# Feed-forward products of a two-block network as seven block products instead of eight, and SBUF tiles at multiples of 256 bytes

## The chip, the cores and the metric

The kernel runs on one core of a Trainium2 chip. The metric is the device time of one execution in microseconds (us), the median over the runs; lower is better.

## The reference, cut to what matters

The network is a block of state-space scan, attention and routed experts, followed by a second block of pooling, a second state-space mixer and a feed-forward part. All of it is float32 over 1024 tokens of 1024 channels. The change touches the very end:

```python
D_FF = 2816
def swiglu(h, w_gate, w_up, w_down):
    return (jax.nn.silu(h @ w_gate) * (h @ w_up)) @ w_down
...
h = h + jnp.concatenate([y_pool, y_ssm], axis=-1) @ w_out
h = h + swiglu(rmsnorm(h, norm_ffn), w_gate, w_up, w_down)
return rmsnorm(h, norm_final)
```

## The kernel before, in words

Float32 products are made on TensorE from operands in `float32r`. Each operand is split into a high part (a rounded copy, by ScalarE) and a low part (the operand minus its high part, by VectorE or GpSimd), and `mm3` (L194) issues three matmuls, high by high, high by low and low by high, into one PSUM bank. A product of a 128x128 block by 512 columns is so three matmuls of 128x512.

`out2` (L2341) is the last stage. Its first half, under `es2`, multiplies the mixer's output by `w_out` for two column halves `n`, adds the residual into `h` (eight row tiles of 128 tokens, in SBUF all the time), forms the mean square (`rms_part`, L1908), scales (`un`), and `split_T` (L1942) transposes each row tile into `hH` and `hL`: 8 blocks of 128 channels by 1024 tokens, high and low. These are the moving operand of what follows.

The second half is the feed-forward part. It takes the 22 column blocks in 11 pairs (`G = 2`). For each block `f`, `gate_up(f)` loads gate and up weights (two DMAs of 512 KB), splits them with the norm's gain folded in (ScalarE writes `gh`, VectorE `gl`), and 96 matmuls (2 token halves, gate and up, 8 channel blocks, 3 each) fill the banks `gu0` and `gu1`. ScalarE applies Silu, VectorE multiplies, ScalarE and GpSimd split the result into `xh` and `xl`. After a pair, 96 matmuls of the down product (8 row tiles, 2 column halves, 2 blocks, 3 each) go to `dn`, and VectorE adds each bank into `h` (L2438). In the last pair the final norm follows each row tile, and the rows leave by DMA.

So each token half sees the full product: gate and up take 22 x 96 = 2112 matmuls, down 11 x 96 = 1056.

The order of the work on each engine is fixed when the program is built: a list scheduler takes the instructions by the order of the source, and lets a later one go first where an earlier one waits for a buffer or an operand. A tile's buffers are a ring (`bufs`), and a new tile waits until the old one's readers are done. All loads of this stage are issued by SyncE's queue (SP), in order: a DMA that waits holds up those behind it.

`Lined` (L113) rounds the size of every SBUF tile up to a multiple of `LINE = 128` bytes, so that tiles start at multiples of 128 bytes. In the addresses that the program before was given, the tiles `h3H` and `h3L` start 128 bytes past a multiple of 256, while `gh`, `gl`, and the down product's `xh`, `xl`, `wh`, `wl` start at a multiple of 256. In the first half of `out2` `wh` and `wl` lie 128 past and `yh`, `yl` at a multiple; in the projection of the first block, `wh`, `wl`, `hH` and `hL` all lie 128 past.

Of the kernel before, what the change touches and what calls it, by code (L numbers as in the profile page):

```python
# [9 lines left out]
BF = mybir.dt.bfloat16  # L10
F = mybir.dt.float32
R = mybir.dt.float32r
# [9 lines left out]
D = 1024  # L22
# [13 lines left out]
def host_arrays(inp):  # L36
# [40 lines left out]
    col("norm_ffn", g["norm_ffn_2"][0].reshape(8, 128).T)  # L77
# [5 lines left out]
    put("ffn_gu", np.stack([g["w_gate_2"][0].reshape(8, 128, 22, 128), g["w_up_2"][0].reshape(8, 128, 22, 128)], 3).transpose(2, 1, 0, 3, 4))  # L83
# [29 lines left out]
class Lined:  # L113


    LINE = 128

    def __init__(self, pool):
        self.pool = pool

    def tile(self, shape, dtype, **kw):
        n, per = int(np.prod(shape[1:])), self.LINE // mybir.dt.size(dtype)
# [6 lines left out]
        return t.rearrange(f"p ({' '.join(names)}) -> p {' '.join(names)}", **dict(zip(names, shape[1:])))  # L129


class LinedContext:
# [8 lines left out]
    @contextmanager  # L141
    def tile_pool(self, **kw):
        with self.tc.tile_pool(**kw) as pool:
            yield pool if kw.get("space") in (PS, DR) else Lined(pool)


class Kernel:
# [60 lines left out]
    def run(self):  # L208
        nc, tc = self.nc, self.tc
        es = self.es  # L210
        with es:
            self.cst = es.enter_context(tc.tile_pool(name="cst", bufs=1))

            es.enter_context(tc.tc.tile_pool(name="edge", bufs=1, side="right")).tile([128, 8], F, name="edge")
# [2126 lines left out]
    def out2(self, y_es):  # L2341
        nc, tc, A = self.nc, self.tc, self.A
        V = nc.vector
        es = ExitStack()
        with es:
            pool = lambda name, bufs=1, **kw: es.enter_context(tc.tile_pool(name=name, bufs=bufs, **kw))
            hp = pool("h3", reuse_waits="tile")
            h = hp.tile([128, NB, D], F, name="h3")
            hH, hL = hp.tile([128, 8, L], R, name="h3H"), hp.tile([128, 8, L], R, name="h3L")
            ss = hp.tile([128, NB], F, name="ss")  # L2350
            gp = pool("ff_g", reuse_waits="tile")
            o_g = self.off["norm_ffn"][0]

            def gate_up(f, more=None):

                out = []
                for i in range(2):
                    st = gp.tile([128, 4, 256], F, name="gst", bufs=2)
                    nc.sync.dma_start(st, A["ffn_gu"][f].rearrange("p k g c -> p k (g c)")[:, 4 * i:4 * i + 4, :])
                    ring = (more, 1) if (2 * f + i) % 3 == 2 else (gp, 2)  # L2360
# [9 lines left out]
            with es2:  # L2370
# [3 lines left out]
                for n in range(2):  # L2374
                    s = slice(512 * n, 512 * n + 512)
                    wt = [self.wsplit(A["w_out_2"][k][:, s], whp, wlp, wsp, 512) for k in range(8)]
                    if n == 1:
                        g0 = gate_up(0)
# [105 lines left out]
```

## Time and profile before

| what | value |
|---|---|
| median of 3 runs | 2865.01 us (2856.89 to 2865.08) |
| the profiled execution's own time | 2855.95 us |
| its span | 2854.2 us |
| mean granted TensorE clock | 0.958 |
| busy in the span | PE 92%, PEld 72%, DVE 61%, ACT 44%, POOL 34% |
| DMA | 263.17 MB, mean 92 GB/s |

PE is TensorE's matmuls, PEld its weight loads, DVE VectorE, ACT ScalarE, POOL GpSimd. A matmul's busy time overlaps with the next one's, so the pace of the matmuls is read from the starts of successive ones, not from the time of one. The span runs from the first to the last instruction; the execution's own time is 1.75 us longer. "L196" is line 196 of the kernel; the three lines of `mm3` are L196, L197 and L198, and the names behind them tell the product apart.

### The profile page before, as it was taken

Reading aid. Unit: us, or ns where it says so; the run is one execution under the profiler, and the core shown is the slowest. Engines: PE = TensorE matmul, PEld = TensorE weight load, DVE = VectorE, ACT = ScalarE, POOL = GpSimd, SP = SyncE. Lnnn points to the kernel's source line nnn. Section 1 sums busy time; section 2 is a strip of 40 time slices with the busy share of each in tenths; the row PEclk is TensorE's granted clock in tenths of the full one; section 3 lists DMA queues with packets and bytes.
Section 4 is the critical chain, followed back from the end, with each engine's and each line's share of the span. In section 5 each row is a group of like instructions: output and inputs, shape, how many; then the busy total and the mean of one; then the engine's idle time right before and its main releaser. Section 6 shows DMA issues by size and latency. Waiting matters only on the chain.

```text
span 2854.2 us, 35834 instructions
## 1 busy us (share of the span) xinstructions
PE 2630.8 (92%) x12713; PEld 2067.2 (72%) x12713; DVE 1740.4 (61%) x3505; ACT 1260.7 (44%) x2748; POOL 968.3 (34%) x1059
## 2 busy tenths in 40 slices
PE   7799999988989999998979996869999999999998
PEld 4676788745777777777757775647878888888886
DVE  7655576797578898885566777596343333333334
ACT  3233444456369999983234553405341221111212
POOL 5522011273046666663344551044321111111111
PEclk9999999997999999999959998978999999999999
DMA  7555411001510000004167886311221111111111
GB/s 262 182 191 199 142 49 39 31 1 66 192 49 20 16 16 16 16 30 132 74 204 198 261 253 222 112 37 45 89 74 45 45 51 53 45 45 45 46 36 59
DMA packets 100388, 263.17 MB, mean 92 GB/s; under 512 B 16128, under 2 KB 36272, under 8 KB 91344
## 3 DMA queue, kind: packets, MB, share of 16 engines
q1 hardware_dynamic: 57792, 149.53, 15.2%
q0 software_dynamic: 14848, 70.67, 8.2%
q10 hardware_dynamic: 27568, 40.67, 4.2%
q8 instruction: 101, 1.65, 0.2%
q14 instruction: 79, 0.65, 0.1%
HBM read 212.55 MB, written 57.70 MB: 95 GB/s over the span
## 4 chain that ended last, share of the span: by engine, by line
PE 63%; DVE 16%; DMA 7%; ACT 6%; issue 5%; POOL 2%; SPq 0%; ACTq 0%; POOLq 0%; DVEq 0%
PE gu L196 6%; PE gu L198 6%; PE gu L197 6%; PE S L1116 4%; PE mm L196 4%; PE mm L197 4%; PE mm L198 4%; PE pt L1175 4%; PE dn L197 3%; PE dn L196 3%; PE dn L198 3%; ACT P L1151 2%; DMA u<-yo,tab 2%; PE pv L1196 2%; PE pv L1197 2%
## 5 line engine op out<-in xcount | busy, mean ns | idle before, releaser
L196 PE MATMUL gu<-h3H,gh 128*128 128x512 f32 x704 | 279.0, 396 | 0.0
L198 PE MATMUL gu<-h3H,gl 128*128 128x512 f32 x704 | 278.7, 396 | 0.0
L197 PE MATMUL gu<-h3L,gh 128*128 128x512 f32 x704 | 278.7, 396 | 0.0
L1184 DVE TENSOR_TENSOR pl<-pt,ph 128x512 fp32r<-128x512 f32 x320 | 219.2, 686 | 51.5 <-ACT ph L1180 46.2
L1151 ACT ACTIVATE P<-S,hd 128x512 f32<-128x512 f32 (+1 forms) x384 | 237.6, 622 | 1.8 <-DVE hd L1136 1.8
L1166 POOL TENSOR_SCALAR P<-P,hd 128x512 f32<-128x512 f32 (+1 forms) x256 | 201.8, 801 | 91.0 <-DVE hd L1164 86.4
L1116 PE MATMUL S<-kS,qS 128*128 128x512 f32 (+1 forms) x768 | 211.5, 372 | 19.0 <-ACT P L1151 19.0
L1180 ACT CAST ph<-pt 128x512 fp32r<-128x512 f32 x320 | 187.4, 586 | 28.2 <-PE pt L1175 15.2
L1175 PE MATMUL pt<-consts,P 128*128 128x128 f32 x1280 | 192.9, 273 | 6.5 <-DVE pl L1184 5.4
L2365 DVE SCALAR_TENSOR_TENSOR gl<-gst,vcol,gh 128x256 fp32r<-128x256 f32 x176 | 93.2, 580 | 169.3 <-ACT gh L2364 168.5
L202 POOL TENSOR_TENSOR xl<-sa,xh 128x512 fp32r<-128x512 f32 x44 | 58.0, 1319 | 406.2 <-ACT xh L2427 406.2
L1175 PEld LDWEIGHTS pt<-consts,P 128*128 128x128 f32 x1280 | 156.5, 140 | 45.1 <-DVE pl L1184 9.2
L1129 DVE TENSOR_REDUCE mx<-S 128x1 f32<-128x512 f32 x256 | 173.9, 680 | 2.9 <-PE S L1116 2.2
L2438 DVE TENSOR_TENSOR h<-h,dn 128x512 f32<-128x512 f32 x176 | 119.6, 684 | 89.7 <-PE dn L198 89.7
L964 POOL TENSOR_TENSOR wl<-wst,wh 128x1024 fp32r<-128x1024 f32 (+1 forms) x42 | 84.6, 2024 | 264.3 <-ACT wh L963 263.8
L1116 PEld LDWEIGHTS S<-kS,qS 128*128 128x128 f32 x768 | 128.5, 190 | 63.0 <-ACT P L1151 42.8
L2426 DVE TENSOR_TENSOR sa<-sa,gu 128x512 f32<-128x512 f32 x44 | 30.2, 686 | 234.0 <-PE gu L198 234.0
L197 PEld LDWEIGHTS gu<-h3L,gh 128*128 128x128 f32 x704 | 132.7, 189 | 32.1
L196 PEld LDWEIGHTS gu<-h3H,gh 128*128 128x128 f32 x704 | 132.8, 189 | 32.0
L198 PEld LDWEIGHTS gu<-h3H,gl 128*128 128x128 f32 x704 | 132.6, 188 | 32.1
L1196 PE MATMUL pv<-ph,vS 128*128 128x512 f32 x320 | 150.5, 470 | 1.7 <-ACT ph L1180 1.1
L581 DVE SCALAR_TENSOR_TENSOR acc<-cv,vcol,acc 128x254 f32<-128x254 f32 (+5 forms) x288 | 110.2, 433 | 53.0 <-ACT acc L583 50.5
(690 smaller groups left out, 6941.8 us busy)
## 6 DMA issues: line engine op xcount, KB each, us to landing
gst<-in_ffn_gu_dram SPq DMA_DIRECT2D x44, 512.0 KB, 3.5
wmod<-in_w_mod_dram ACTq DMA_DIRECT2D x64, 256.0 KB, 3.8
wst<-in_ffn_down_dram SPq DMA_DIRECT2D x22, 512.0 KB, 3.9
wst<-in_w_in_dram SPq DMA_DIRECT2D x40, 256.0 KB, 4.0
wmod<-in_w_mod_a_dram SPq DMA_DIRECT2D x8, 1024.0 KB, 5.2
qT<-qt ACTq DMA_DIRECT2D x16, 512.0 KB, 4.3
wst<-in_w_out_dram SPq DMA_DIRECT2D x16, 512.0 KB, 5.4
qS<-qT SPq DMA_DIRECT2D x8, 1024.0 KB, 4.9
```

The source lines that it names most:

```text
L196: nc.tensor.matmul(out, lh, rh, start=first, stop=False)
L197: nc.tensor.matmul(out, lh, rl, start=False, stop=False)
L198: nc.tensor.matmul(out, ll, rh, start=False, stop=last)
L1116: nc.tensor.matmul(S[:, o:o + z - a], qS[b][:, 4 * j + 2 * p + e, :], kS[4 * m + j][:, a:z], start=m == 0, stop=m == 1)
L1129: V.tensor_reduce(m[:, k // 3, k % 3:k % 3 + 1], bank[n], axis=AX.X, op=OP.max)
L1151: nc.scalar.activation(x, bank[n][:, o:o + z - a], AF.Exp, bias=neg[h], accum_out=tot[h][:, i:i + 1])
L1166: nc.gpsimd.tensor_scalar(P[h, half], P[h, half], r[:, 0:1], 1.0, op0=OP.mult, op1=OP.mult)
L1175: nc.tensor.transpose(pt[:, i, :], P[4 * g + i, int(c > 3)][:, o:o + 128], self.ident)
L1180: nc.scalar.copy(split[n][1], split[n][0])
L1184: V.tensor_sub(split[n][2], split[n][0], split[n][1])
L1196: nc.tensor.matmul(pv, v, ph, start=c == 0, stop=False)
L2438: V.tensor_add(x[:, s], x[:, s], ps)
```

## The change

Gate, up and down are each cut into 2 x 2 blocks and computed by seven block products in Winograd's form of Strassen's scheme. For gate and up, the left matrix has the rows (gate, up) of one column block and the columns (channels 0 to 511, 512 to 1023); the right one is the normed input with the channels and the token halves. For down, the left matrix is the hidden layer cut by token half and by column block of a pair, and the right one `w_down` cut by block of a pair and by output half.

- `out2` keeps only its first half. The gain of the norm moves from the weights into `un` (one scalar_tensor_tensor of 128x1024 instead of a tensor_scalar). The transposed input goes into four pairs of tiles `B[i, n]`. `h` is stored to DRAM (`h3`), one DMA of 512 KB per row tile.
- `ffn_hidden` runs blocks 0 and 1 with the eight products (`plain`), and during these forms the sums of input blocks (`sums`, `third`: 48 VectorE operations of 128x512). Blocks 2 to 21 run `operands` and `seven`. Every second block, `pair` forms the left sums for down on GpSimd and stores seven operands (256 KB each), and `weights` loads two rows of `w_down` blocks, forms the right sums on GpSimd and stores them.
- `ffn_out` loads for each of the seven products and each of the 11 pairs two operands of 256 KB, splits them, and accumulates over the 11 pairs in four banks; the banks are then added into the row tiles `y`, which start as `h3`.
- The layout of `ffn_gu` in DRAM changes so that each of the four blocks of a column block is one DMA of 256 KB.
- `Lined.LINE` becomes 256 for every SBUF tile of the kernel; tiles of up to 2048 bytes that are no multiple of it go to a pool of their own, which is filled up to a multiple.

```diff
 class Lined:
-    LINE = 128
+    LINE = 256
+    SMALL = 2048
...
+        if n % per and n * size <= self.SMALL:
+            self.taken[kw["name"]] = kw.get("bufs", self.bufs) * -(-n * size // 32) * 32
+            return self.small.tile(shape, dtype, **kw)
...
 def out2(self, y_es):
-                                V.tensor_scalar(un, x, r, None, op0=OP.mult)
-                                self.split_T(pp, un, hH, hL, t, 2)
+                                nc.sync.dma_start(self.h3[t], x)
+                                V.scalar_tensor_tensor(un, x, r, gain, op0=OP.mult, op1=OP.mult)
+                                turned(un, t)
...
+    def ffn_split(self, x, pool):
+        hi, lo = (pool.tile([128, 4, 128], R, name=n) for n in ("gh", "gl"))
+        flat = lambda t: t.rearrange("p a b -> p (a b)")
+        self.nc.scalar.copy(flat(hi), x)
+        self.nc.vector.tensor_sub(flat(lo), x, flat(hi))
+        return hi, lo
...
+            bp, yp, gy, pp = pool("ff_b"), pool("ff_y"), pool("ff_h", 4), pool("ff_ps", 8, space=PS)
+            T = {t: [bp.tile([128, 4, 512], R, name=f"t{t}{x}") for x in "hl"] for t in (1, 2, 4)}
+            T[3] = B[0, 1]
+            def product(ps, op, b, first, last):
+                for k in range(4):
+                    self.mm3(ps, op[0][:, k, :], op[1][:, k, :], b[0][:, k, :], b[1][:, k, :], first and k == 0, last and k == 3)
...
+            def operands(f):
+                a11, a21, a12 = (self.ffn_raw(f, gp, *gi) for gi in ((0, 0), (1, 0), (0, 1)))
+                a22 = self.ffn_raw(f, gy, 1, 1, bufs=1)
+                s2, s3 = buf("s2"), buf("s3")
+                ops = {}
+                ops[1] = self.ffn_split(a11, gy)
+                V.tensor_sub(s3, a11, a21)
+                V.tensor_sub(s2, a22, s3)
+                ops[6] = self.ffn_split(s2, gp)
+                ops[7] = self.ffn_split(s3, gy)
+                V.tensor_add(a21, a21, a22)
+                ops[5] = self.ffn_split(a21, gp)
+                ops[2] = self.ffn_split(a12, gy)
+                ops[4] = self.ffn_split(a22, gp)
+                V.tensor_sub(s2, a12, s2)
+                ops[3] = self.ffn_split(s2, gy)
+                return ops
+            def seven(f, ops):
+                y = [buf(f"h{f % 2}{n}") for n in range(2)]
+                p1, u2, u3, x = (buf("u", 8) for _ in range(4))
...
+                nc.scalar.copy(p1, prod(1, B[0, 0]))
+                V.tensor_add(u2, p1, prod(6, T[2]))
+                V.tensor_add(u3, u2, prod(7, T[3]))
+                m5 = prod(5, T[1])
+                V.tensor_add(u2, u2, m5)
+                V.tensor_add(x, u3, m5)
+                V.tensor_add(p1, p1, prod(2, B[1, 0]))
+                nc.scalar.activation(p1, p1, AF.Silu)
+                V.tensor_add(u3, u3, prod(4, T[4]))
+                V.tensor_mul(y[0], p1, u3)
+                V.tensor_add(u2, u2, prod(3, B[1, 1]))
+                nc.scalar.activation(u2, u2, AF.Silu)
+                V.tensor_mul(y[1], u2, x)
+                return y
+            def pair(i, h0, h1):
+                (a11, a21), (a12, a22) = h0, h1
+                nc.gpsimd.tensor_sub(s3, a11, a21)
+                nc.gpsimd.tensor_add(a21, a21, a22)
+                nc.gpsimd.tensor_sub(s2, a22, s3)
+                nc.gpsimd.tensor_sub(s4, a12, s2)
+                for p, x in enumerate((a11, a12, s4, a22, a21, s2, s3)):
+                    nc.sync.dma_start(self.hop[11 * p + i][:], x)
+            def weights(i):
...
+            for f in range(2, 22):
+                ops = operands(f)
+                if f % 2 == 0:
+                    i = f // 2 - 1
+                    pair(i, hid.pop(f - 2), hid.pop(f - 1))
+                    weights(i)
+                hid[f] = seven(f, ops)
...
+    def ffn_out(self):
+            sp, op = pool("fd_s", 6), pool("fd_o", 11)
...
+            def operands(p, i):
...
+                nc.scalar.copy(hi, st)
+                V.tensor_sub(lo, st, hi)
...
+            for t in range(NB):
+                nc.sync.dma_start(y[t], self.h3[t])
+            product(1, (0, 1), (1, 0), (1, 1), (0, 0))
+            product(6, (0, 1), (1, 0), (1, 1))
+            product(5, (0, 1), (1, 1))
+            product(3, (0, 1))
+            product(2, (0, 0))
+            for t in range(4):
+                final(t)
+            product(7, (1, 0), (1, 1))
...
```

Product 4 comes last; it runs row tile by row tile, each followed by the final norm of that tile.

## Rows read from the trace of the kernel before

**Rows 1.** The page: busy tenths of TensorE in 40 slices of the span.

```profile
PE   7799999988989999998979996869999999999998
```

**Rows 2.** Stretches: busy us (instructions) of PE, PEld, DVE, ACT, POOL; clock, DMA share, GB/s.

```profile
2200.00:2300.00 100.00, 100.00 (x434) 81.27 (x433) 33.72 (x57) 19.28 (x38) 12.68 (x9) 1.00 0.15 48
...
2000.00:2010.00 10.00, 10.00 (x44) 8.10 (x43) 4.31 (x7) 2.55 (x4) 0.14 (x1) 1.00 0.87 318
2100.00:2110.00 10.00, 5.91 (x20) 4.78 (x19) 5.97 (x16) 4.63 (x10) 0.44 (x1) 0.67 0.71 227
```

**Rows 3.** Timeline of PE: start, duration (us), operands; one pair of the feed-forward part.

```profile
2307.49 0.40 PE L196 MATMUL gu<-h3H,gh 128*128 128x512 f32 x1
...
2352.29 0.39 PE L196 MATMUL dn<-wh,xh 128*128 128x512 f32 x1
...
2374.06 0.40 PE L196 MATMUL gu<-h3H,gh 128*128 128x512 f32 x1
```

**Rows 4.** The same of unbroken runs: 102 matmuls of a projection, 93 of out2.

```profile
136.29 0.40 PE L196 MATMUL mm<-wh,hH 128*128 128x512 f32 x1
...
159.23 0.39 PE L198 MATMUL mm<-wh,hL 128*128 128x512 f32 x1
...
2048.74 0.39 PE L196 MATMUL mm<-wh,yh 128*128 128x512 f32 x1
...
2070.11 0.40 PE L198 MATMUL mm<-wh,yl 128*128 128x512 f32 x1
```

**Rows 5.** Groups, 2200 to 2790 us: busy us, mean ns; idle before, releaser.

```profile
L2438 DVE TENSOR_TENSOR h<-h,dn 128x512 f32<-128x512 f32 x144 | 98.0, 685 | 78.2 <-PE dn L198 78.2
L202 POOL TENSOR_TENSOR xl<-sa,xh 128x512 fp32r<-128x512 f32 x36 | 47.7, 1324 | 334.7 <-ACT xh L2427 334.7
L2425 ACT ACTIVATE sa<-gu 128x512 f32<-128x512 f32 x35 | 20.9, 597 | 144.2 <-PE gu L198 144.2
L963 ACT CAST wh<-wst 128x1024 fp32r<-128x1024 f32 x18 | 18.0, 1050 | 171.8 <-PE dn L198 171.8
```

**Rows 6.** Groups of DVE over the whole span: two inputs in SBUF, 512 and 1024 columns.

```profile
L1611 DVE TENSOR_TENSOR gul<-wst,guh 128x1024 fp32r<-128x1024 f32 x64 | 75.7, 1222 | 40.7 <-ACT guh L1610 39.3 <-DMA s_k<-oT 1.2
...
L2390 DVE TENSOR_TENSOR yl<-yc,yh 128x512 fp32r<-128x512 f32 x16 | 11.0, 692 | 27.2 <-ACT yh L2389 27.1
```

**Rows 7.** Timeline of DVE and of POOL around 1993 us.

```profile
1993.65 1.75 DVE L2336 TENSOR_TENSOR yc<-yc,th 128x512 f32<-128x512 f32 x1
...
1993.56 1.29 POOL L964 TENSOR_TENSOR wl<-wst,wh 128x512 fp32r<-128x512 f32 x1 [0.23 <-ACT wh L963]
```

**Rows 8.** Timeline of DVE: the next block's weights and the product of the current block.

```profile
2327.60 1.69 DVE L2365 SCALAR_TENSOR_TENSOR gl<-gst,vcol,gh 128x256 fp32r<-128x256 f32 x4 [7.96 <-ACT gh L2364]
2330.16 0.69 DVE L2426 TENSOR_TENSOR sa<-sa,gu 128x512 f32<-128x512 f32 x1 [0.87 <-PE gu L198]
```

**Rows 9.** One DMA issue of SP (start, us), and issues: count, size, us to landing.

```profile
2106.35 0.33 SPq L2359 DMA_DIRECT2D gst<-in_ffn_gu_dram  x1
...
wst<-in_w_in_dram SPq DMA_DIRECT2D x40, 256.0 KB, 4.0
```

**Rows 10.** Timeline at the start of the feed-forward part.

```profile
2103.48 0.75 DVE L2401 TENSOR_SCALAR gst<-h,rr 128x1024 f32<-128x1024 f32 x1
...
2105.97 0.78 PE L196 MATMUL gu<-h3H,gh 128*128 128x512 f32 x1
...
2108.68 0.63 PE L196 MATMUL gu<-h3H,gh 128*128 128x512 f32 x1
```

**Rows 11.** The end: timeline, and the group of the final norm's squares.

```profile
2840.55 0.40 PE L198 MATMUL dn<-wh,xl 128*128 128x512 f32 x1
...
2848.32 0.20 ACT L187 ACTIVATE qs<-rv 128x1 f32<-128x1 f32 x1 [3.82 <-DVE rv L2446]
...
2849.50 1.42 DVE L2458 SCALAR_TENSOR_TENSOR wst<-h,qo,gfin 128x512 f32<-128x512 f32 x2
...
L2444 ACT ACTIVATE junk<-h 128x1024 bf16<-128x1024 f32 x4 | 4.2, 1053 | 3.9 <-DVE h L2438 3.2 <-DVE qr L188 0.7
```

More of the change, by code (lines that the diff above doesn't have):

```diff
@@ L129, in tile, with fill @@
         return t.rearrange(f"p ({' '.join(names)}) -> p {' '.join(names)}", **dict(zip(names, shape[1:])))
+    def fill(self):
+        rest = -sum(self.taken.values()) % self.LINE
+        if rest:
+            self.small.tile([128, rest // 4], F, name="fill", bufs=1)
 class LinedContext:
@@ L2343, in out2 @@
         V = nc.vector
+        self.h3 = self.dram.tile([NB, 128, D], F, name="h3d")
         es = ExitStack()
         with es:
[L2346 to L2360, printed above, removed]
-                    gh, gl = (ring[0].tile([128, 4, 256], R, name=x, bufs=ring[1]) for x in ("gh", "gl"))
-                    for k in range(4):
-                        gm = self.vcol[:, o_g + 4 * i + k:o_g + 4 * i + k + 1]
-                        nc.scalar.activation(gh[:, k, :], st[:, k, :], AF.Copy, scale=gm)
-                        V.scalar_tensor_tensor(gl[:, k, :], st[:, k, :], gm, gh[:, k, :], op0=OP.mult, op1=OP.subtract)
-                    out.append((gh, gl))
-                return out
+            hp = es.enter_context(tc.tile_pool(name="h3", bufs=1, reuse_waits="tile"))
+            B = {(i, n): [hp.tile([128, 4, 512], R, name=f"b{i}{n}{x}") for x in "hl"] for i, n in ((0, 0), (1, 0), (1, 1), (0, 1))}
+            gp = es.enter_context(tc.tile_pool(name="ff_g", bufs=3, reuse_waits="tile"))
             es2 = ExitStack()
@@ L2373, in out2, with turned @@
                 wsp, whp, wlp = pool2("o2_s", 2, reuse_waits="tile"), pool2("o2_h", 8, reuse_waits="tile"), pool2("o2_l", 8, reuse_waits="tile")
+                h = wp.tile([128, NB, D], F, name="h3")
+                ss = wp.tile([128, NB], F, name="ss")
+                gain = self.row(wp, "gain", A["norm_ffn"])
+                def turned(x, t):
+                    for i in range(2):
+                        pt = pp.tile([128, 4, 128], F, name="tp", bufs=2)
+                        for j in range(4):
+                            k = 4 * i + j
+                            nc.tensor.transpose(pt[:, j, :], x[:, 128 * k:128 * k + 128], self.ident)
+                        hi, lo = (b[:, :, 128 * (t % 4):128 * (t % 4) + 128] for b in B[i, t // 4])
+                        nc.scalar.copy(hi, pt)
+                        V.tensor_sub(lo, pt, hi)
                 for n in range(2):
```

210 lines of the change are left out of this document (146 added, 64 removed).

## The prediction, made blind

> **What bounds the kernel now.** I read the busy slices of the page first: from the slice at about 1930 us TensorE stands at nine tenths up to the last slice [rows 1]. The stretches in numbers come next: in 100 us of the feed-forward part PE is busy for all of it at the full clock (1.00, the 2.4 GHz level), while VectorE has 34 us, ScalarE 19, GpSimd 13, and DMA a share of 0.15 [rows 2]. No other engine sets the pace there, so a matmul taken out gives back its own spacing. That spacing is read from the starts of matmuls [rows 3]: 192 gate and up matmuls take 2352.29 - 2307.49 = 44.80 us, 0.2333 each, and the 96 of down 2374.06 - 2352.29 = 21.77 us, 0.2268 each. Both are 128x512 in the same type and at the same clock. In sum, 2112 x 0.2333 + 1056 x 0.2268 = 732.2 us; from the first of these matmuls at 2105.97 [rows 10] to the start of the last at 2840.55 [rows 11] there are 734.6. The missing 2.4 us lie at the start: six intervals from 2105.97 to 2108.68 take 2.71 us instead of 1.40 [rows 10], at the lower clock after PE stood idle for some 4 us (granted 0.67 over that stretch, [rows 2]). After the last matmul's start 13.65 us remain to the end of the span.
>
> **Why two spacings.** By the addresses of the program before, gate and up stream `h3H` and `h3L` (128 bytes past a multiple of 256) against weights at a multiple; down has both at a multiple. Two other runs separate the address from the product [rows 4]: with both operands 128 past, 101 intervals take 22.94 us, 0.2271 each; with the moving one 128 past and the other at a multiple, 92 intervals take 21.37 us, 0.2323 each. Equal residues run at 0.227, unequal ones at 0.232 to 0.233. With `LINE = 256` all large tiles have residue 0, so I take 0.2268 for every matmul of the new stage; the other end is 0.2333.
>
> The Trainium skill, "SBUF — State Buffer", section "Who interferes with whom", speaks against this: PE never waits on anyone there, and it has independent read ports for the two operands. By that rule an address could not matter, and gate and up would keep 0.2333. The rows of this trace side with the address, but by two pairs only; that is a rival below.
>
> **The change, part by part.**
>
> *Matmuls.* Gate and up: 2 blocks x 96 + 20 x 7 products x 12 = 192 + 1680 = 1872. Down: 7 products x 11 pairs x 4 tiles x 3 = 924. In all 2796 for 3168. At 0.2268: 634.1 us for 732.2, so -98.1 (fewer matmuls give -84 to -87 of it, the spacing the rest).
>
> *Supply of a block of gate and up.* Its 84 matmuls take 19.05 us. VectorE has 4 sums, 7 low parts and 9 steps from the banks: 20 x 0.69 [rows 5, 6] = 13.8 us. ScalarE has 7 copies, one evacuation and 2 Silu: 10 x 0.60 [rows 5] = 6.0. Both lie under the 19.05, provided that the operands of a block are made while the one before it multiplies. The rings allow that: seven split operands stand in rings of four and three, in the order of the products, so the first of the next block can be split when product 1 of this one is done. That the scheduler uses such room is seen in [rows 8]: `gl` of the next block runs 2.6 us before the last multiplication of the current one, although it stands later in the source. So cost 0; with the cover gone it is the slower rival below.
>
> *GpSimd.* Per pair of blocks 8 sums of 128x512 at 1.32 [rows 5] = 10.6 us of 38.1. Two results meet a deadline: the store of `a21` must have landed before `y[1]` of the next block overwrites it, 19 us after the last product of the pair; three sums (4 us), the issue and the landing (4.0, [rows 9]) leave over 10 us. Cost 0, bounds 0 and the rival on the port.
>
> *SP's queue.* Per pair of blocks 8 loads, 7 stores and 4 larger transfers, 19 issues of 0.33 us [rows 9] in 38 us, 6.0 MB, 158 GB/s. In the down part two loads of 256 KB per four tiles' 12 matmuls (2.72 us): 193 GB/s. The trace has moved 318 GB/s in a stretch [rows 2]. A store that waits for GpSimd holds up the loads behind it, at most for the 10.6 us of the sums; the raw weights are a block ahead of their use, so nothing of it reaches PE.
>
> *Start.* `un` as a two-input operation takes 1.22 [rows 6] for 0.75 [rows 10] on the last tile's chain: +0.5. During blocks 0 and 1 (43.5 us of PE) VectorE has 48 operations of sums, 4 multiplications, 5 low parts and 11 operations of block 2: 68 x 0.69 = 46.9 us, 0.61 to 0.65 each where they run back to back. Bounds 0 and 8 us of stall at block 2; I take 2, near the difference.
>
> *Into down.* The first six operand buffers lie where `B[0,0]` and `B[1,0]` lay, free after products 1 and 2 of the last block, so the first pairs are loaded before its end. The row tiles (8 x 512 KB = 4.2 MB, 13 us at 318 GB/s) stand ahead of the later operands in SP's queue. With six pairs (16 us of PE) loaded, bounds are 0 and 9 us (a load of 4.0, copy 1.05 and low part 1.22 [rows 5, 6], and some 2 us at the low clock); I take 4. Within down VectorE has per product 11 low parts x 1.22 + 8 additions x 0.69 = 18.9 of 29.9 us: cost 0.
>
> *End.* Before, the last pair ends on four row tiles whose norms queue on VectorE. Now each of the last four tiles has 33 matmuls, 7.5 us, so only the last tile's chain stands behind PE: addition 0.69, square 1.05 [rows 11], 1.4 for the mean square and the root (1.2 of it from 2848.32 to 2849.50), two products with the gain 1.42, 3.3 from their end to the end of the span [rows 11], 0.39 of the last matmul and 0.7 of hand-overs: 9.0 for 13.65, so -4.7.
>
> *The stages ahead.* The 384 matmuls of `out2`'s first half go from 0.2323 to 0.2268: -2.1. For other stages the new addresses and the new order of buffers may do either; I take 0, bounds -10 and +8.
>
> Sum: 2105.97 - 2.1 + 0.5 + 634.1 + 2.4 + 2 + 4 + 9.0 = 2755.9 us of span, and 1.75 around it: 2757.6, 98 us under the profiled execution's 2855.95. That execution lies 9.1 us under the median (two of three runs are at 2865, one at 2857), so I add a little: 2760.
>
> **The rivals.**
>
> *The port of GpSimd and VectorE binds.* In [rows 7] an operation of VectorE with two SBUF inputs takes 1.75 us instead of 0.69, begun 0.09 us after one of GpSimd that takes 1.29. Eleven of a block's 20 VectorE operations have two SBUF inputs. If each of the 8 GpSimd sums held VectorE throughout, a pair of blocks would need 27.6 + 10.6 = 38.2 us of VectorE against 38.1 of PE: no slack left. Then half a hold (0.65) reaches PE per sum: 8 x 0.65 x 10 pairs = 52 us as a ceiling, 26 as a middle: 2786, up to 2812. For it: the collision is in the trace. Against: nine operations read PSUM, and the operands stand a block ahead. The Trainium skill has the rule, same page and section: the two-input operation and the GpSimd one exclude each other for the whole instruction. The trace agrees with it (1.75 for 0.69).
>
> *The address does nothing.* Then gate and up cost 1872 x 0.0065 = 12 us more and `out2` keeps its 2: 2774.
>
> *The operands are not made ahead: slower.* If VectorE takes a block's sums and splits only behind the last evacuation of the block before, PE waits at each of 20 blocks for addition 0.69, Silu 0.60, multiplication 0.69, copy 0.60 and low part 0.69 = 3.3 us, some 1.5 more at products 6 and 5, and pays the low clock afterwards, 2.0 [rows 10]: 6.8 x 20 = 136 us: 2896. The gain is 98 us, 4.9 per block, and above that the change loses. For it: the rings are just seven deep, and `s2` has a single buffer for two of the operands. Against: [rows 8].
>
> **How the numbers follow.** Forecast 2760: 0.63, its own range 2740 to 2780. Port: 0.15. Address: 0.12. Operands late: 0.10, nearly all of it slower. The range 2738 to 2815 holds the first three and leaves out the last. One measurement tells no change from 0.3% (8.6 us) or more; so faster 0.90, same 0.02, slower 0.08.
>
> **What would show it.** Matmuls of gate, up and down all 0.227 apart; about 425 us from the first matmul of block 0 to the last of block 21, and 210 for down; PE at 1.00 in both but for gaps of some us at block 2 and at the first of down; VectorE at about 0.7 of the hidden part; 9 us behind the last matmul. Gaps at each block would be the late operands, gaps beside GpSimd's sums the port, a spacing of 0.233 the address.

## The result and the profile after

The changed kernel takes 2810.36 us (median of 4 runs, 2808.94 to 2832.09), the kernel before 2861.34 beside it (4 runs, 2856.89 to 2865.08). The ratio is 0.9843, 95% interval 0.9808 to 0.9878. It is 51 us or 1.6% faster where the prediction had 100 us, though 2810 lies inside the range given. The profiled run takes 2809.2 us with a span of 2807.3, of which 51.4 are more than the 2755.9 of the prediction's sum.

Execution times of one kernel spread here by up to 33 us. In the profiles of after and its variants the feed-forward part begins anywhere from 2101.6 to 2132.1 us, so much of the spread arises ahead of it (last section). So the parts are compared by their own length, from the start of the first feed-forward matmul to the end of the span: 748.2 us before (2105.97 to 2854.2), 701.9 after (2105.47 to 2807.3), 651.5 in the forecast.

TensorE's busy tenths on the page, in answer to [rows 1]:

```profile
PE   7899999998999999998978996887987999997998
```

Slices 31 (from 2105 us) and 37 (from 2527 us) stand at seven tenths, where before has nine. The stretches, with the columns of [rows 2]:

```profile
2100.00:2150.00 50.00, 46.12 (x196) 38.33 (x197) 28.52 (x37) 10.43 (x19) 24.76 (x17) 0.91 0.60 215
2150.00:2200.00 50.00, 29.75 (x101) 21.60 (x99) 34.25 (x50) 12.74 (x23) 34.54 (x15) 0.78 0.50 173
...
2300.00:2400.00 100.00, 100.00 (x443) 82.82 (x442) 80.21 (x112) 33.58 (x57) 19.84 (x12) 1.00 0.36 116
...
2565.00:2620.00 55.00, 38.64 (x136) 29.48 (x135) 24.36 (x23) 22.82 (x23) 4.69 (x3) 0.81 0.91 330
2650.00:2750.00 100.00, 100.00 (x442) 82.80 (x442) 63.52 (x87) 44.56 (x50) 0.00 (x0) 1.00 0.60 199
```

Where PE is busy for all of the stretch, 443 matmuls go into 100 us for 434 before [rows 2]. VectorE takes 80 us of 100 there for 34. Two stretches are far from full: 2150 to 2200, where GpSimd is busy for 34.5 of 50 us, and 2565 to 2620, where the DMA engines have a share of 0.91 and move 330 GB/s.

The 2796 matmuls of the part are 0.2267 us apart wherever they follow each other closely (2704 intervals of 0.2267 on average). What an interval takes beyond that is called lost here: a wait, or a matmul at a lower clock behind one (the two stretches above have a granted clock of 0.78 and 0.81; behind the waits matmuls are 0.43 apart). In after 59.9 us are lost, for 8.4 in the forecast (2.4 + 2 + 4): 1.9 in block 0, 0.0 in block 1, 21.2 in block 2, 8.8 in block 3, 3.3 in blocks 4 to 21, 4.9 in the step into down, 19.8 in down's first product, and nothing in the six products behind it.

**Blocks 2 and 3.** What PE waited for from 2150 to 2260 (us in total, times, longest), the last row from 2564 to 2620:

```profile
PE m L217 <- DVE gl L2434: 8.0, 3, 5.4
PE m L215 <- ACT gh L2433: 7.0, 2, 6.1
PE m L215 <- ACT t2h L2481: 5.6, 1, 5.6
...
PE a L215 <- ACT oh L2609: 16.1, 3, 8.2
```

The late operands are split parts (`gh`, `gl`) and the sum of right operands `t2`. VectorE makes `gl` and the sums that ScalarE then rounds to `gh` and `t2h`, and GpSimd's timeline shows what stands beside it:

```profile
2137.50 1.29 POOL L2562 TENSOR_TENSOR d<-d 128x512 f32<-128x512 f32 x1 [5.36 <-DMA d<-in_ffn_down_dram]
...
2163.16 9.55 POOL L2562 TENSOR_TENSOR d<-d 128x512 f32<-128x512 f32 x1 [4.80 <-DMA d<-in_ffn_down_dram]
2172.78 7.13 POOL L2563 TENSOR_TENSOR d<-d,d 128x512 f32<-128x512 f32 x1
...
2182.93 1.29 POOL L2550 TENSOR_TENSOR h<-h,h 128x512 f32<-128x512 f32 x1
```

`d` are the down weights of `weights(i)`. Nothing in them depends on the hidden layer, so they did not stay where the loop has them: all eleven sets run from 2100 to 2257 us, by the end of block 5 (one of the expectations below says nine of eleven; it is all). VectorE's timeline:

```profile
2106.83 0.68 DVE L2388 TENSOR_TENSOR b11l<-tp,b11h 128x512 fp32r<-128x512 f32 x1
2118.54 0.69 DVE L2498 TENSOR_TENSOR h<-u,m 128x512 f32<-128x512 f32 x1 [11.03 <-PE m L217]
...
2122.23 0.69 DVE L2472 TENSOR_TENSOR u<-b01h,b01l 128x512 f32<-128x512 f32 x1
...
2136.96 0.68 DVE L2482 TENSOR_TENSOR t2l<-u,t2h 128x512 fp32r<-128x512 f32 x1
2137.56 1.78 DVE L2479 TENSOR_TENSOR u<-u,b10l 128x512 f32<-128x512 f32 x1
2139.27 1.78 DVE L2472 TENSOR_TENSOR u<-b01h,b01l 128x512 f32<-128x512 f32 x1
...
2183.84 0.68 DVE L2535 TENSOR_TENSOR u<-u,m 128x512 f32<-128x512 f32 x1
2197.42 0.69 DVE L2509 TENSOR_TENSOR s<-gst 128x512 f32<-128x512 f32 x1 [12.89 <-DMA gst<-in_ffn_gu_dram]
```

Three things are to be seen. The right operand is complete at 2107.5, but the first sum of it (L2472) runs at 2122.2: it stands in VectorE's fixed order behind block 0's product `h` (L2498), which waits 11 us for PE. From 2137.5, beside GpSimd, an operation takes 1.78 us for 0.68, as in [rows 7]. And the wait works in the other direction too: at 2163 to 2180, where VectorE has operation behind operation, GpSimd's two take 9.55 and 7.13 for 1.29. SP's queue shows what follows:

```profile
2158.81 2.78 SPq L2560 DMA_DIRECT2D d<-in_ffn_down_dram  x2
2179.93 3.38 SPq L2567 DMA_DIRECT2D wop<-d  x2
...
2192.18 1.88 SPq L2427 DMA_DIRECT2D gst<-in_ffn_gu_dram  x3
```

The store of `d` (`wop`) waits for GpSimd until 2179.9, and the loads of block 3's weights (`gst`) stand behind it until 2192.2. VectorE waits 12.89 us for them, and PE 6.5 at 2193.7.

**Into down.** SP's queue, then ScalarE's copies of the operands:

```profile
2564.18 0.32 SPq L2554 DMA_DIRECT2D hop<-h  x1
2564.60 0.38 SPq L2606 DMA_DIRECT2D st<-hop  x1
...
2567.40 1.71 SPq L2554 DMA_DIRECT2D hop<-h  x2
2572.30 0.80 SPq L2554 DMA_DIRECT2D hop<-hs  x2
2573.14 0.45 SPq L2607 DMA_DIRECT2D st<-in_ffn_down_dram  x1
...
2575.34 6.87 SPq L2648 DMA_DIRECT2D y<-h3d  x8
2583.19 0.32 SPq L2606 DMA_DIRECT2D st<-hop  x1
```

```profile
2568.85 1.04 ACT L2609 CAST oh<-st 128x1024 fp32r<-128x1024 f32 x1 [2.20 <-DMA st<-in_ffn_down_dram]
2577.02 1.04 ACT L2609 CAST oh<-st 128x1024 fp32r<-128x1024 f32 x1 [7.13 <-DMA st<-in_ffn_down_dram]
2580.09 1.05 ACT L2609 CAST oh<-st 128x1024 fp32r<-128x1024 f32 x1 [2.02 <-DMA st<-in_ffn_down_dram]
2593.56 1.04 ACT L2609 CAST oh<-st 128x1024 fp32r<-128x1024 f32 x1 [12.43 <-DMA st<-in_ffn_down_dram]
```

The first load of an operand (`st`) is issued at 2564.6, when block 21 issues its last matmuls: SP stood at a store of that block's `y[0]` (`hop<-h`). The two loads of the second pair are parted by four more stores of the last pair. After the third pair come the eight row tiles, and the fourth pair's operand is copied at 2593.56, 12.4 us after ScalarE was free for it.

**The end.** In answer to [rows 11], the last matmul and the last tile's products with the gain:

```profile
2798.98 0.39 PE L217 MATMUL a<-oh,ol 128*128 128x512 f32 x1
...
2802.74 1.41 DVE L2632 SCALAR_TENSOR_TENSOR un<-y,qo,gfin 128x512 f32<-128x512 f32 x2
```

From the last matmul's start to the end of the span it is 8.35 us for 13.65.

### The profile page after: what moved, and what is told of

Read it like the earlier page. It is cut to its first block, busy times and chain, and to the rows that moved or that the text cites. A ratio compares the mean times of both kernels' runs of the same rounds, so it can differ in the third digit from the quotient of the medians.

```text
span 2807.3 us, 36195 instructions
## 1 busy us (share of the span) xinstructions
PE 2550.4 (91%) x12341; PEld 2007.4 (72%) x12341; DVE 1976.1 (70%) x3707; ACT 1324.0 (47%) x2762; POOL 1002.0 (36%) x1078
## 5 line engine op out<-in xcount | busy, mean ns | idle before, releaser
L1135 PE MATMUL S<-kS,qS 128*128 128x512 f32 (+1 forms) x768 | 211.7, 373 | 18.2 <-ACT P L1170 18.2
L2610 DVE TENSOR_TENSOR ol<-st,oh 128x1024 fp32r<-128x1024 f32 x77 | 92.8, 1221 | 65.9 <-ACT oh L2609 62.0
L215 PE MATMUL a<-oh 128*128 128x512 f32 x308 | 122.3, 400 | 16.1 <-ACT oh L2609 16.1
L1216 PE MATMUL pv<-pl,vS 128*128 128x512 f32 x320 | 126.8, 396 | 0.2 <-DVE pl L1203 0.2
L216 PE MATMUL a<-ol,oh 128*128 128x512 f32 x308 | 122.7, 398 | 0.2 <-DVE ol L2610 0.2
L217 PE MATMUL a<-oh,ol 128*128 128x512 f32 x308 | 122.2, 397 | 0.0
L216 PE MATMUL mm<-wl,hH 128*128 128x512 f32 x288 | 114.6, 398 | 1.4 <-DVE wl L255 1.1
L215 PE MATMUL mm<-wh,hH 128*128 128x512 f32 x288 | 115.5, 401 | 0.0
L217 PE MATMUL mm<-wh,hL 128*128 128x512 f32 x288 | 113.5, 394 | 0.0
L217 PE MATMUL cv<-hH,wl 128*128 128x512 f32 (+1 forms) x288 | 104.2, 362 | 1.0 <-POOL wl L584 1.0
L215 PE MATMUL cv<-hH,wh 128*128 128x512 f32 (+1 forms) x288 | 105.0, 364 | 0.0
```

The costliest lines, as they stand in the source:

```text
L215: nc.tensor.matmul(out, lh, rh, start=first, stop=False)
L216: nc.tensor.matmul(out, lh, rl, start=False, stop=False)
L217: nc.tensor.matmul(out, ll, rh, start=False, stop=last)
L1135: nc.tensor.matmul(S[:, o:o + z - a], qS[b][:, 4 * j + 2 * p + e, :], kS[4 * m + j][:, a:z], start=m == 0, stop=m == 1)
L1216: nc.tensor.matmul(pv, v, pl, start=False, stop=c == NBT - 1)
```

## The experiments

The table gathers what the profiles show: the length from the first feed-forward matmul to the end, and the us lost by stretch (as above, beyond 0.2267 us between the starts of matmuls; in shifted the 6.1 of blocks 4 to 21 are the wider spacing and no waits).

| kernel | length | blocks 0, 1 | 2 | 3 | 4 to 21 | step | 1st product | behind PE |
|---|---|---|---|---|---|---|---|---|
| forecast | 651.5 | 2.4 | 2 | 0 | 0 | 4 (both) | | 9.0 |
| after | 701.9 | 1.9 | 21.2 | 8.8 | 3.3 | 4.9 | 19.8 | 8.3 |
| sums_early | 692.5 | 9.0 | 9.1 | 0 | 9.8 | 4.3 | 17.9 | 8.8 |
| weights_held | 686.9 | 0.7 | 10.2 | 0 | 9.8 | 10.9 | 13.6 | 8.3 |
| weights_queue | 708.8 | 2.0 | 14.8 | 21.4 | 5.5 | 4.7 | 18.2 | 8.5 |
| no_weights | 671.9 | 2.1 | 5.2 | 0 | 0 | 4.5 | 18.1 | 8.5 |
| vector_sums | 666.0 | 0.7 | 4.0 | 0 | 0 | 4.5 | 14.9 | 8.3 |
| rows_late | 693.7 | 2.0 | 18.4 | 8.1 | 1.2 | 4.4 | 7.6 (+10.2 in the 2nd) | 8.3 |
| quarters | 693.7 | 1.8 | 14.8 | 21.1 | 1.5 | 4.5 | 7.6 | 8.9 |
| pool_stores | 682.8 | 1.5 | 20.8 | 8.7 | 1.7 | 2.5 | 5.8 | 8.2 |
| all_three | 655.7 | 1.9 | 4.1 | 0 | 0 | 2.5 | 5.0 | 8.7 |
| shifted | 660.9 | 2.5 | 2.0 | 0.3 | 6.1 | 2.6 | 5.2 | 8.7 |
| last_steps | 648.6 | 1.8 | 0 | 0 | 0 | 2.5 | 2.5 | 8.2 |

**The addresses alone (line_only).** The kernel before with the changed allocator:

```diff
-    LINE = 128
+    LINE = 256
...
+        if n % per and n * size <= self.SMALL:
...
+            return self.small.tile(shape, dtype, **kw)
```

> The kernel before, with tiles at multiples of 256 bytes and nothing else of the change (same products, same order). The address theory: the 2112 gate and up matmuls go from 0.2333 to 0.2268 us apart and the 384 of the first half of the output product before them from 0.2323 to 0.2268, 13.7 + 2.1 = 16 us in all, so some 2845 for 2861 (ratio 0.9945), with spacings of 0.227 everywhere. The rival, that the spacing belongs to the product and not to the addresses: 0.2333 stays, ratio 1.000.

Measured: 2833.13 us (2832.17 to 2835.74), ratio 0.9916 (0.9883 to 0.9949). The part takes 733.5 us for 748.2: 14.7 less, and the gate and up matmuls are 0.2273 apart on average. From the first matmul of out2 to the feed-forward part 127.3 us pass for 129.4, the 2.1 expected. Of the rest of the 25 us, 7 lie ahead of out2 in the profiled runs, before 1830 us; whether the addresses or the spread between executions gave them is open. The address theory holds: with the products of before, the allocator alone gives 14.7 us in the part, for the 46.3 of all of after.

**The sums of the right operands first (sums_early).**

```diff
-            hid[0] = plain(0, four(0, g0))
-            g1 = four(1, self.ffn_three(1, gp))
+            f0 = four(0, g0)
             sums(t3)
+            hid[0] = plain(0, f0)
+            g1 = four(1, self.ffn_three(1, gp))
```

> The kernel after, with the sums of the right operands ordered ahead of block 0's products (and of block 1's splits), so that VectorE begins them when the last transposed tile is complete, at about 2108 and not at 2122. If VectorE's order is the cause, most of block 2's 21 us goes: 14 to 21 us gained, 2790 to 2796, and block 3 keeps its gap. If GpSimd's early sums on the port are the cause, the sums start earlier but run at 1.75 us beside GpSimd, and the gain is 0 to 7 us.

Measured: 2811.83 us (2795.15 to 2817.02), ratio 0.9819 (0.9774 to 0.9864): no gain that can be told from after. Block 2 loses 12 us less, but 7 appear in blocks 0 and 1 and 7 in blocks 4 to 21. In the part's length 9.4 us are gained, and block 3's gap, expected to stay, is gone. With GpSimd at work the order moves the loss rather than taking it away.

**The weights held back (weights_held).** Each `weights(i)` is ordered behind the stores of its pair:

```diff
-                    pair(i, hid.pop(f - 2), hid.pop(f - 1))
-                    weights(i)
+                    last = pair(i, hid.pop(f - 2), hid.pop(f - 1))
+                    with tc.issue_after(getattr(last, "ins", last)):
+                        weights(i)
```

> The kernel after, with the weights' sums of each pair held until that pair's hidden stores are issued, instead of nine of eleven sets running from 2096 to 2257 us. In after, blocks 2 and 3 and the four behind them lose 21.2 + 8.8 + 3.4 = 33 us. If GpSimd's early sums (they share the port with VectorE) and their waiting stores in SP's queue are the cause, the gap of 6.5 us behind the loads of block 3 goes, and the multiplications of block 2 wait for shorter operations of VectorE: 12 to 25 us gained, 2785 to 2798. If the cause is only that VectorE begins the sums of the right operands 15 us late, in its fixed order, then block 2 still loses some 15 to 20 us and the gain is 8 us at most (block 3).

Measured: 2792.28 us (2783.74 to 2794.65), ratio 0.9761 (0.9724 to 0.9797), inside the first theory's span. Block 3's gap is gone and block 2's is halved. But 9.8 us appear in blocks 4 to 21, all from block 12 on, and the step into down costs 10.9: the last pair's weights stand ahead of down's first loads. GpSimd's sums cost wherever they run.

**Whose queue (weights_queue).** The weights' sums as early as in after, their loads and stores on GpSimd's own queue:

```diff
-                    nc.sync.dma_start(d[x], A["ffn_down"][2 * i + x])
+                    nc.gpsimd.dma_start(d[x], A["ffn_down"][2 * i + x])
...
-                    nc.sync.dma_start(self.wop[i][x], d[x])
+                    nc.gpsimd.dma_start(self.wop[i][x], d[x])
```

> The kernel after with the loads and stores of the down weights' sums on GpSimd's queue, the sums themselves on GpSimd and as early as in after. It separates the two ways in which the hoisted sums can cost: SP's queue no longer waits for them, the port still does. If SP's blocked queue is what costs, the gap of block 3 (8.8 us) and a part of block 2's 21.2 go: 685 to 693 for 701.9. If the port alone costs, block 2 keeps its 15 to 21 us, and block 3's gap goes only if it was the queue: 690 to 702.

Measured: 2815.48 us (2 runs), length 708.8: neither theory. Block 3's gap did not go, it grew to 17.5 us. What SP waited for from 2160 to 2220:

```profile
SPq L2554 <- DVE h L2498: 23.6, 2, 23.4
SPq L2554 <- POOL h L2550: 23.0, 1, 23.0
```

The second row is the store of a hidden sum, L2550. GpSimd has it behind its stretched weights' sums (11.83 and 7.13 us here), and the loads of block 3 stand behind that store. So the chain starts on the port and passes through two queues in order, GpSimd's and SP's. Taking one kind of store out of SP's queue does not cut it.

**Without the weights' sums (no_weights).** Products 4 to 7 of down read the raw weights, and loads, sums and stores of `weights` are left out:

```diff
             def weights(i):
-                d = [yp.tile([128, D], F, name=f"d{x}") for x in range(2)]
-                ...
+                pass
```

> The kernel after with the sums of the down weights left out (their loads, their four GpSimd operations a pair and their stores; products 4 to 7 of down read the raw weights instead, so this part of the computation is missing). It bounds what this path costs. Measured from the first feed-forward matmul to the end of the span (701.9 us in after), since the stages ahead vary by up to 26 us between executions. If GpSimd on the port and the waiting stores in SP's queue cause the losses of blocks 2 to 7 (33 us) beyond what the late start of VectorE's sums costs, 15 to 25 us go: 677 to 687. If VectorE's order alone sets block 2, at most block 3's 9 us go: 693.

Measured: 2775.23 us (2 runs), length 671.9, below the range given for the first theory. All 30 us go in blocks 2 to 21 (33.3 to 5.2) but for some 2 in the first product. The other theory, that VectorE's order alone sets block 2, is left with 5 us. This run takes the sums off the port and out of the queue at once and doesn't part the two.

**The sums on VectorE (vector_sums).** weights_held, with all eight sums of a pair on VectorE:

```diff
-                nc.gpsimd.tensor_sub(s3, a11, a21)
+                V.tensor_sub(s3, a11, a21)
...
-                nc.gpsimd.tensor_sub(b11, b12, b11)
+                V.tensor_sub(b11, b12, b11)
```

> The kernel with the held weights (686.9 us from the first feed-forward matmul to the end), and all eight sums of a pair on VectorE instead of GpSimd. VectorE gets 8 x 0.61 = 4.9 us more per pair of blocks, 38 us. If the port is what stretches the hidden part (an operation of 0.68 takes 1.78 beside one of GpSimd, 8 of which would cost VectorE up to 8.8 us a pair), this is no dearer: no operation of VectorE takes 1.78, and the gaps of 9.8 us in blocks 10 to 21 and part of block 2's 10.2 go: 670 to 682. If VectorE is simply too full, the gaps grow at every second block: 10 x 1 to 3 us more, 695 to 715.

Measured: 2775.49 us (2772.68 to 2798.38), ratio 0.9735 (0.9671 to 0.9798); the length is 666.0, better than expected. VectorE has more to do and PE waits less. The group of the split's low parts from 2300 to 2500 us (count, busy us, mean ns), first weights_held, then vector_sums:

```profile
L2434 DVE TENSOR_TENSOR gl<-gst,gh 128x512 fp32r<-128x512 f32 x40 | 44.2, 1104 | 0.0
```

```profile
L2434 DVE TENSOR_TENSOR gl<-gst,gh 128x512 fp32r<-128x512 f32 x43 | 29.4, 684 | 0.0
```

The same operation takes 0.68 us on the average for 1.10. Four such sums cost VectorE 2.7 us; beside GpSimd four sums cost it up to 4 x 1.1 = 4.4 in stretched operations, and held up their readers as well.

**The row tiles later (rows_late).** All eight behind the operands of the first product:

```diff
+                if p == 1:
+                    for t in range(NB):
+                        nc.sync.dma_start(y[t], self.h3[t])
                 add(m, *to)
```

> The kernel after, with the eight row tiles (4.2 MB) loaded behind the operands of the first product of down instead of ahead of its pairs 3 to 10. In after this product loses 19.8 us and the step into it 4.9. If the row tiles in SP's queue hold the operands up, the gaps in the middle of the product (3.7 and 8.6 us and the low clock behind them) go: 10 to 17 us gained, 2793 to 2800. If the lateness comes from the first operands alone, whose loads are issued behind the last pair's stores, the gain is 0 to 4 us.

Measured: 2813.01 us (2806.45 to 2824.17), ratio 0.9856 (0.9816 to 0.9896); 8.2 us less in the part, between the two theories. The first product loses 12 us less, and the second loses 10.2. The stretches of the two, and the 20 us in which the row tiles are on their way, with the columns of [rows 2]:

```profile
2564.00:2606.00 42.00, 34.54 (x134) 25.97 (x133) 16.25 (x15) 13.31 (x14) 4.62 (x3) 0.92 0.89 326
2606.00:2647.00 41.00, 33.06 (x138) 26.89 (x137) 34.43 (x39) 20.95 (x20) 0.00 (x0) 0.92 0.81 287
...
2590.00:2610.00 20.00, 17.87 (x79) 14.46 (x77) 9.36 (x13) 7.12 (x8) 0.00 (x0) 1.00 0.99 379
```

Beside the row tiles the DMA engines have a share of 0.99. By an estimate from the sizes, a product's operands (5.8 MB) and the row tiles (4.2 MB) are 10 MB, some 330 GB/s over the 29.9 us of a product.

**The row tiles by quarters (quarters).** Down in the order 2, 3, 5, 1, 6, 7, 4, with one quarter (1 MB) of the rows loaded in each of the first four products:

```diff
+                    if i == 8 and rows:
+                        r, n = rows
+                        for t in range(4 * r, 4 * r + 4):
+                            nc.sync.dma_start(y[t][:, 512 * n:512 * n + 512], self.h3[t][:, 512 * n:512 * n + 512])
...
-            product(1, (0, 1), (1, 0), (1, 1), (0, 0))
...
+            product(2, (0, 0), rows=(0, 0))
+            product(3, (0, 1), rows=(0, 1))
+            product(5, (0, 1), (1, 1), rows=(1, 1))
+            product(1, (0, 1), (1, 0), (1, 1), (0, 0), rows=(1, 0))
```

> The kernel after with the products of down in the order 2, 3, 5, 1, 6, 7, 4, and the row tiles loaded a quarter (1 MB) a product, where each quarter is first added to. After loses 24.7 us in the step into down and its first product, and loading the rows later but all at once moved 10.2 us of that into the second product with the DMA engines at a share of 0.99. If the 4.2 MB of row tiles beside the operands are more than DMA moves in that time, 10 to 18 us go: 684 to 692 from the first feed-forward matmul to the end. If only the last pair's stores ahead of the first loads matter, the loss stays within 4 us of what it is: 698 to 702.

Measured: 2816.51 us (2801.59 to 2827.63), ratio 0.9834 (0.9779 to 0.9889), no gain in the whole. Into down the loss falls from 24.7 to 12.1 with nothing in the products behind: 12.6 us, as the DMA theory had it. Block 3's gap took most of it back in the profiled run: it is 18 us there for 6.5, GpSimd's two sums taking 10.76 and 7.13. That gap is the unrepaired chain of block 3, and its size differs between kernels with the same hidden part.

**The last pair's stores (pool_stores).**

```diff
-                    nc.sync.dma_start(self.hop[11 * p + i][:], x)
+                    (nc.gpsimd if i == 10 else nc.sync).dma_start(self.hop[11 * p + i][:], x)
```

> The kernel after with the seven stores of the last pair issued on GpSimd's queue, which leaves SP free to issue the loads of down's first six pairs while the last block still multiplies. If those stores in SP's queue make the first operands late, the step into down falls from 4.9 us to 1 or less and the gap of 3.7 us at pairs 1 and 2 goes, while the row tiles behind the sixth pair still delay pair 6: 8 to 14 us gained of 24.7, 688 to 694 from the first feed-forward matmul to the end. If the operands are late for DMA bandwidth alone, 0 to 3 us.

Measured: 2790.61 us (2783.65 to 2797.31), ratio 0.9759 (0.9707 to 0.9811). Into down 8.4 us are lost for 24.7, 16.3 less and more than expected: five pairs are now loaded and copied in a row from 2566.0, and even with all row tiles ahead of the rest only the sixth pair is late and costs 1.7 us. Both causes are real, and the stores are the larger.

**All three repairs (all_three).** vector_sums, pool_stores and quarters in one kernel.

> Sums of the pairs on VectorE and the weights held (666.0 us from the first feed-forward matmul to the end, of which the step into down and its first product lose 19.4), with the last pair's stores on GpSimd's queue (8.4 lost there alone of 24.7) and the products of down in the order 2, 3, 5, 1, 6, 7, 4 with the row tiles by quarters (12.1 lost there alone). If the two causes of the late operands are separate, 2 to 5 us of the 19.4 are left: 649 to 652, which is the forecast's own part (651.5), and 2751 to 2760 us for a run that starts this part at about 2105. If they share one cause (the DMA rate), 7 us or more are left: 654 or above.

Measured: 2763.81 us (6 runs, 2756.22 to 2788.77), ratio to before 0.9693 (0.9649 to 0.9736). The length is 655.7, with 7.5 of the 19.4 left into down: the number of the second theory. The quarters take only 0.9 off the 8.4 that pool_stores leaves. Two stretches, at block 2 and into down, and what PE waited for from 2528 to 2575:

```profile
2150.00:2170.00 20.00, 17.84 (x72) 14.29 (x71) 18.34 (x31) 6.53 (x12) 0.00 (x0) 0.91 0.56 184
...
2530.00:2570.00 40.00, 35.38 (x145) 28.39 (x144) 25.70 (x27) 22.72 (x23) 2.69 (x5) 0.91 0.98 358
...
PE a L215 <- ACT oh L2612: 2.4, 1, 2.4
PE a L216 <- DVE ol L2613: 2.2, 1, 2.2
```

At block 2 VectorE is busy for 18.3 of 20 us; whether it has too much work there or is late by its order, last_steps tells. Into down the DMA engines are nearly full (share 0.98), but PE waits for no load. ScalarE's and VectorE's timelines show what it waits for:

```profile
2532.76 0.63 ACT L2541 ACTIVATE u<-u 128x512 f32<-128x512 f32 x1 [4.80 <-DVE u L2540]
2533.29 4.82 ACT L2612 CAST oh<-st 128x1024 fp32r<-128x1024 f32 x5
...
2536.08 6.89 DVE L2613 TENSOR_TENSOR ol<-st,oh 128x1024 fp32r<-128x1024 f32 x6
```

The first pair's load goes out at 2515.7, but its copy stands in ScalarE's order behind block 21's last Silu (L2541), which waits 4.8 us for that block, and its low part on VectorE behind the last pair's sums. These two waits are 4.6 of the 7.5 us; most of the rest is matmuls 0.43 apart behind them (granted clock 0.62 from 2534 to 2540). So the number is the second theory's and the cause, the DMA rate, is not.

**The addresses in the new part (shifted).** all_three with a 128-byte filler in front of the right operand's tiles and one behind them:

```diff
+            es.enter_context(tc.tc.tile_pool(name="shift", bufs=1)).tile([128, 32], F, name="shift")
             hp = es.enter_context(tc.tile_pool(name="h3", bufs=1, reuse_waits="tile"))
```

> The kernel with all three repairs (655.7 us from the first feed-forward matmul to the end), with the eight tiles of the right operand moved by 128 bytes and everything else where it was, so that they lie 128 bytes off the weights' residue to 256, and the sums of right operands still on it. If the spacing follows the addresses, the 1152 matmuls that stream the moved tiles (192 of the two plain blocks, 4 of 7 products of the other twenty) are 0.233 apart and the other 720 of gate and up stay at 0.2267: 1152 x 0.0065 = 7.5 us more, 663. If it follows the product or the sharing of the engine, all stay at 0.2267: 656.

Measured: 2763.84 us (2 runs). Intervals that start at a matmul on a moved tile are 0.2321 to 0.2334 us (0.2267 in all_three), those on the sums of right operands 0.2277 to 0.2285. So the spacing follows the addresses; why the second group rose by some 0.001 at all is open. The length is 5.2 us more, not 7.5: block 2 lost 2 us less, with PE slower ahead of it.

**The last steps (last_steps).** all_three, with sums_early's order and the last pair's sums on GpSimd:

```diff
+                E = nc.gpsimd if i == 10 else V
+                E.tensor_sub(s3, a11, a21)
...
+            f0 = four(0, g0)
             sums(t3)
+            hid[0] = plain(0, f0)
```

> The kernel with all three repairs, with the sums of the right operands ordered ahead of block 0's products on VectorE, and the last pair's four sums on GpSimd, which does nothing else by then. All three loses 4.1 us at block 2 and 7.5 at the step into down. If VectorE's order is what is late at block 2 once the port is free, its 4.1 us go; if VectorE has simply more work in blocks 0 to 2 than PE's 62 us cover, the loss moves to block 1 or stays. The last pair's sums stand 2 us ahead of the first low part of down on VectorE, so 1 to 2 us of the 7.5 go. Together 650 to 653 for 655.7; no gain, 656, if the first is only moved.

Measured: length 648.6, 7.1 less than all_three: block 2's 4.1 us are gone without a trace elsewhere, and 2.4 of the 7.5 into down. With GpSimd off the port the order is worth what it was not worth in sums_early, and block 2 was late by VectorE's order and not by too much work. Into down the wait for the low part falls from 2.2 to 0.5 us; the 2.4 for the copy behind the Silu stay. The whole takes 2775.13 us (6 runs, 2753.31 to 2779.04), ratio 0.9696 (0.9667 to 0.9725), the same as all_three: in the profiled run its part begins at 2125.7 us for 2101.6, for the reason in the last section. Both beat the kernel after.

## Why the prediction was right and wrong

The excess of 51.4 us over the sum is all placed: 31.3 in the hidden blocks behind block 1 (33.3 for 2), 20.7 into down (24.7 for 4), 1.1 for the later start, and -1.7 in the other terms.

- *Matmuls* and *why two spacings*: right. 2796 matmuls at 0.2267. All large tiles start 128 bytes past a multiple of 256 and not at one, by the addresses of the program, but the residues are equal, and that is what counts (line_only, shifted). The Trainium skill, "SBUF — State Buffer", section "Who interferes with whom", has PE wait on nobody; these two runs, 0.2273 and 0.233, show an effect of the addresses that the rule has no room for, and the measurement decides.
- *Supply of a block*: right for blocks 8 to 21. VectorE is busy for 80 of 100 us (about 0.7 was expected), and PE waits for nothing. So the slower rival, operands not made ahead, is out.
- *GpSimd* (cost 0) and *SP's queue* ("nothing of it reaches PE"): wrong, and the first failed step. Both took `weights(i)` to run where the loop has it, once per pair. It depends on nothing in the loop, and all eleven sets ran in blocks 0 to 5, on the port and in the queue, where VectorE had the most to do. And the hold of a waiting store was bounded by the 10.6 us of the sums at their own speed; two of them took 16.7. Without the weights' sums 30 us are gone (no_weights). How the loss in the blocks divides between the port and the queue stays open: weights_queue, meant to part them, met both.
- *Start*: the bounds 0 to 8 hold for VectorE's work by itself (5.2 in no_weights, 4.0 in vector_sums), and the value 2 was low; the remaining 4 are VectorE's order, as last_steps shows. In after GpSimd's load came on top.
- The port rival was the right mechanism, but in after it bound at another place: not over eight sums in each of ten pairs, but where VectorE has no idle time. With the eight sums where the loop has them (weights_held) blocks 12 to 21 lose 9.8 us, for the rival's middle of 26, and nothing with the sums on VectorE (vector_sums); so "cost 0" fails there too. The rival's count is off: 13 of a block's 20 operations have both inputs in SBUF and not 11, for the two multiplications read no bank. The cost includes the other direction, VectorE holding GpSimd, which the prediction left out. The Trainium skill, "SBUF — State Buffer", section "Who interferes with whom", calls the shared pair of ports an exclusive lock, which would allow it; the trace shows it with 9.55 for 1.29, much longer than any one operation of VectorE.
- That 2810 lies inside the rival's 2786 to 2812 is luck: 20.7 of the 51.4 us are into down, where the rival had nothing.
- *Into down* (4, bounds 0 to 9): wrong, 24.7. It forgot its own remark that SP's queue is in order: the last pair's stores wait for block 21 and stood ahead of the first loads. And the row tiles were said to cost nothing behind six loaded pairs that were never there in after. The buffers were free as the step said, but late: in pool_stores the first pair's loads go out at 2548.4, behind product 1, the next only at 2559.3, behind product 2, which is the fifth of the seven, 5 us before the block's last matmul. That was enough for five pairs (8.4 left; with quarters 7.5). Of what is left 2.4 us are ScalarE's order, which the sum did not have.
- *End*: right, 8.35 for 9.0.
- *The stages ahead*: the spacing of out2 gave its 2.1 (line_only). In after the last row tile's chain took longer, 4 us by the distance from out2's last `wh` matmul to the first of the new part (10.4 for 6.5), more than the 0.5 of the sum, and the start came out at 2105.5 for 2104.4.

With the queues and the port repaired the part takes 655.7 and 648.6 us, for the forecast's 651.5: the arithmetic of the change was right, and what the fixed order of the queues and engines and the shared port did with it was not.

## What to carry to other kernels

Work that depends on nothing in a loop may not run where the loop has it (here all eleven sets ran in its first six blocks); price it at the place where it can first run, beside the busiest stretch of the engine whose port it shares. A queue in order is priced by its slowest waiting entry at that entry's stretched speed, and the loads that must come first belong ahead of, or on another queue than, stores that wait for the last result. Before giving elementwise work to an idle GpSimd, compare its cost on VectorE with what it stretches there: here eight sums a pair were cheaper on VectorE.

## What the runs showed of the hardware that was not expected

**GpSimd starved.** An operation of 1.29 us took 8.65 to 11.83 on GpSimd beside an unbroken run of VectorE's operations with two inputs in SBUF, in each of the five profiles with this order (after, rows_late, pool_stores, quarters, weights_queue), and the next one 7.12 or 7.13. It is not the weights' sums alone: a hidden sum (L2550) took 7.03 in no_weights. In all five, each of the two ends 1.2 us behind the start of VectorE's first operation with one input in PSUM (`m`); in after these ends are 2172.71 and 2179.91, and VectorE's operations are:

```profile
2171.47 1.27 DVE L2498 TENSOR_TENSOR h<-u,m 128x512 f32<-128x512 f32 x2
...
2178.69 0.68 DVE L2531 TENSOR_TENSOR u<-u,m 128x512 f32<-128x512 f32 x1
```

So GpSimd got through where VectorE took only one input from SBUF.

**A clock that rises or not, 20 us.** Ahead of out2 lies a sparse stretch, and a dense one behind it. PE in these stretches (busy us, count, granted clock, DMA share, GB/s), first of after, then of last_steps:

```profile
1900.00:1920.00 20.00, 5.71 (x17) 0.50 0.00 0
1920.00:1935.00 15.00, 15.00 (x46) 0.50 0.00 0
1935.00:1965.00 30.00, 29.90 (x180) 1.00 0.00 1
```

```profile
1900.00:1920.00 20.00, 5.63 (x14) 0.50 0.03 13
1920.00:1935.00 15.00, 15.00 (x48) 0.50 0.00 0
1935.00:1965.00 30.00, 30.00 (x101) 0.50 0.00 1
```

Both are at the 1.2 GHz level while PE is mostly idle, and both are then busy throughout. In one the clock is back at 2.4 GHz from 1935, in the other it stays low beyond 1965, which makes the part begin some 20 us later. before and all_three go the first way in their profiled runs, sums_early and quarters the second. What decides it is open. That it also makes most of the spread of up to 33 us within one kernel is argued and not shown, for one execution of each was profiled; the longer executions do have the lower mean clock (all_three: 0.944 in the longest, 0.953 in the shortest). It is why a gain of a few us has to be read from the part and not from the whole.
